# Transposing six of eight output blocks on VectorE and by transfers in SBUF, with the gate row in float32r and the norm's constant on GpSimd, in a fused linear-attention block

## The chip, the cores and the metric

One Trainium2 chip, one of its cores. The metric is the time of one execution on the device in microseconds (us), lower is better; a figure of a kernel is the median of its runs. The engines are TensorE (PE, with its weight loads shown apart as PEld), VectorE (DVE), ScalarE (ACT), GpSimd (POOL) and SyncE (SP), which issues nearly all transfers (DMAs).

## The reference

Sequence length, model width and number of rows are 1024 each, all data is float32, and there is one layer: a gated linear attention with a modulated RMS norm ahead of it.

```
c_act = silu(c)
shift, scale, gate = split(c_act @ ada_w + ada_b, 3)
h = rmsnorm(x, norm_g) * (1 + scale) + shift
q, k, v, g_lr, r = split(h @ w_in)            # 512, 512, 1024, 16, 1024 columns
log_a = log_sigmoid(g_lr @ w_alpha + b_alpha) / 16
o = chunked gated linear attention of q, k, v, log_a   # 4 heads of 256 values
o = rmsnorm(o, norm_g of the head) * silu(r)
x = x + gate * (o @ w_out)
return rmsnorm(x, final_g)
```

## The kernel before

Matrix products of float32 data are made of three float32r products: each operand is split into a rounded high part and the rest (`hi = Copy(x)` on ACT, `lo = x - hi` on DVE or POOL), and hi\*hi, hi\*lo and lo\*hi are accumulated (`PAIRS`, line 424). Most of the kernel's small engine work is such splitting.

The program has three stages. First the modulation, the transposed and split h (`hh0` to `hh7`, `hl0` to `hl7`, one pair for each 128 columns of h), and the projection to q and k. Then 32 steps, s = 0 to 31 (line 958): each is one tile of 128 rows times a quarter of the columns of v and r, 24 main matmuls of 512 columns (272 and 256 for s under 8, where the decay's columns ride along). Step s also carries, by `hooks` (line 881), pieces of the attention of earlier steps: chunk n = s - 4 of 128 rows of one head goes through `gla_at`, `gla_kv`, `gla_o` and `gla_og`; the exponentials of two chunks go through `e_head` to `e_kt`. Then 16 steps, s = 32 to 47, make the output: step 32 + t multiplies row tile t of o by the first half of w_out's columns, step 40 + t by the second, 24 main matmuls of 512 columns each (the last step in two halves), followed by the residual sum and the final norm.

o is collected in eight output blocks `OG[b]` of 128 x 4 x 256: block b holds four row tiles of one head, so head b // 2, rows 512 (b % 2) on. `gla_o` (line 797) sums a chunk's squares on ACT into `oss`, DVE multiplies by 1/256 and adds epsilon, POOL raises to the power -1/2 into `ors`, and `gla_og` (line 810) multiplies the chunk by that and by silu(r), which lies in the block already.

`o_tr(t)` (line 858) makes the transposed and split tile t for the output: eight 128x128 transposes on PE into two banks of PSUM, two copies of 512 columns on ACT (`hh`), two subtractions on DVE (`hl`). It overwrites `hh`t and `hl`t of the projection, which step 31 reads last, so it starts in step 31 at the earliest, and step 32 + t waits for it. Ahead of those steps w_out's pieces are loaded into `raw`, `wa` and `qk` slots, scaled on DVE by the head's norm weights and the gate row (`scale_piece`, line 616) and split (`conv_piece`).

The gate row `GB` (tile `wg`) is summed over eight pieces in 128 partitions by DVE; `gate_bc` (line 850) then sums over the partitions and spreads the row, with one full float32 matmul against a matrix of ones for each half, in steps 5 and 7, and a copy back on DVE.

The order of the instructions isn't that of the code: class `Program` collects them, gives each a latest start by estimated costs, and issues a list-scheduled order on each engine (`schedule`, line 129). Each engine then runs its list in that order. Almost every instruction is therefore recorded at line 217, and the rows are told apart by their tiles.

Of the kernel before, what the change touches and what calls it, by code (L numbers as in the profile page):

```python
# [8 lines left out]
F32R = mybir.dt.float32r  # L9
U8 = mybir.dt.uint8  # L10
AF = mybir.ActivationFunctionType
ALU = mybir.AluOpType
# [4 lines left out]
EPS = 1e-6  # L17
# [8 lines left out]
class Program:  # L26
# [37 lines left out]
    def cost(self, e, m, out, ins, kw):  # L64
        n = 1
        for d in out.shape[1:]:
            n *= d
        psum = any(a.space == bass.MemoryType.PSUM for a in ins + [out])
        if m == "dma_start":
            return n * out.shape[0] * 4 / 360e3  # L70
        if e == "pe":
            if m == "transpose":
                return 0.11
            k = 1 if ins[0].dtype == F32R else 4
            return 0.0135 + n * k / 2400 if n > 1 else 0.22
        if e == "act":
            return (0.05 if psum else 0.09) + n / 1200 + (0.2 if "accum_out" in kw else 0) + \
                (0.095 * sum(hasattr(kw.get(a, 0), "tensor") for a in ("scale", "bias")))
        if e == "dve":
            fast = m in ("tensor_copy", "tensor_scalar", "memset") and not psum  # L80
            return (0.13 if "scalar" in m else 0.068) + n * (0.52 if fast else 1.042) / 1000
        if m != "tensor_tensor":
            return 0.08 + n * 0.8 / 1000
        return 0.46 if kw.get("op") == ALU.pow else 0.11 + n * 2.1 / 1000
# [144 lines left out]
def gla_block(ctx, tc, x, c, ada_w, ada_b, norm_g, w_in, w_alpha, b_alpha, gn_g, w_out, final_g, out):  # L229
    nc = tc.nc  # L230
    prog = Program(nc)
# [220 lines left out]
    def gate_w_load():  # L452
# [5 lines left out]
        for q0 in (0, 32, 96):  # L458
            sync.dma_start(war[q0:q0 + 16, :], w_alpha[0])

    def gate_w_conv():
        war = W["a"]
        act.activation(WA, war, AF.Copy)
        dve.tensor_tensor(WA[32:64, :], war[32:64, :], f(WA[32:64, :]), op=ALU.subtract)
# [217 lines left out]
    oss = T("oss", [128, 32])  # L682
    ors = T("ors", [128, 32])

    OG, X, SHL, KD = {}, {}, {}, {}

    def c4(ap):
        return ap.rearrange("p (c i) -> p c i", i=64)
# [108 lines left out]
    def gla_o(n):  # L797
        u, s = n // 2, n % 2
        p = P(("m4", "m5")[n % 2 if n > 2 else 0])
        PO[n] = p  # L800
        inter = n % 8 != 0
        if inter:
            mm3(p[:, :256], [X[u][i][:, 640 + 128 * s:768 + 128 * s] for i in range(2)],
                [SHL[n][:, i, :] for i in range(2)], last=False)
        mm3(p[:, :256], ATH[n], vt(n), first=not inter)
        act.activation(p[:, 256:512], p[:, :256], AF.Square, accum_out=oss[:, n:n + 1])
        dve.tensor_scalar(oss[:, n:n + 1], oss[:, n:n + 1], 1.0 / 256, EPS, op0=ALU.mult, op1=ALU.add)
        pool.tensor_tensor(ors[:, n:n + 1], oss[:, n:n + 1], mh[:, 0:1], op=ALU.pow)

    def gla_og(n):  # L810
        og = OG[n // 4][:, n % 4, :]
        dve.scalar_tensor_tensor(og, PO[n][:, :256], ors[:, n:n + 1], og, op0=ALU.mult, op1=ALU.mult)

    def og_tag(b):
        return f"wa{12 + b}" if b < 2 else f"qk{b // 2 - 1}{1 - b % 2}"
# [29 lines left out]
    def gate_acc(i):  # L845
        kk, j = i // 2, i % 2
        g = GB[:, 512 * j:512 * j + 512]
        dve.scalar_tensor_tensor(g, GA[i], cact[:, kk:kk + 1], g, op0=ALU.mult, op1=ALU.add)

    def gate_bc(i):  # L850
        p = P("tr")
        pe.matmul(p, ones, GB[:, 512 * i:512 * i + 512], start=True, stop=True)
        dve.tensor_copy(GB[:, 512 * i:512 * i + 512], p)


    OT = {}

    def o_tr(t):
        oh = T(f"hh{t}", [128, 8, 128], F32R)
        ol = T(f"hl{t}", [128, 8, 128], F32R)  # L860
        OT[t] = (oh, ol)
        for g in range(2):
            p = P(("tr", "md")[g])
            for i in range(4):
                e = 4 * g + i
                src = OG[(e // 2) * 2 + t // 4][:, t % 4, 128 * (e % 2):128 * (e % 2) + 128]
                pe.transpose(p[:, 128 * i:128 * i + 128], src, ident)
            hi = oh[:, 4 * g:4 * g + 4, :].rearrange("p a b -> p (a b)")
            lo = ol[:, 4 * g:4 * g + 4, :].rearrange("p a b -> p (a b)")
            act.activation(hi, p, AF.Copy)  # L870
            dve.tensor_tensor(lo, p, f(hi), op=ALU.subtract)

    XRT = ["qk31", "G", "qk30", "wa7", "wa4", "wa5", "wa14", "wa8"]
    XR, FS = {}, {}
# [6 lines left out]
    def hooks(s):  # L881
        H = {}

        def at(k, fn, *a):
            H.setdefault(k, []).append((fn, a))
# [50 lines left out]
        if s < 5:  # L936
            for i in range(4):
                if s > 0:
                    at(i, gate_acc, 4 * (s - 1) + i)
                if s < 4:  # L940
                    at(4, gate_load, 4 * s + i)
            if s == 0:
                at(0, gate_init)
        if s == 5:
            at(0, gate_bc, 0)
        if s == 7:
            at(0, gate_bc, 1)
        if s >= 31 and s < 39:
            at(4 if s == 31 else 1, o_tr, s - 31)
        if s >= 32 and s < 40:  # L950
# [101 lines left out]
```

## Time and profile before

| | us |
|---|---|
| median of 3 runs (lowest to highest) | 454.27 (453.81 to 457.32) |
| the profiled execution, its own time | 455.46 |
| its span in the profile | 453.7 |

The span runs from the program's first recorded instruction to its last; 1.8 us lie outside it. The profile's page gives busy time by engine, the chain of work that ended last, and groups of instructions with their count, busy time and mean duration in ns. Views of the trace give the same for any stretch. A busy engine isn't the bound for that alone: what counts is what waits for what. Ends of matmuls are modelled, so the distance from one start to the next is the better measure of a matmul.

### The profile page before, as it was taken

The page shows a single profiled execution, that of the slowest core. Times are in us where ns is not written, and L with a number is a line of the kernel's source. Part 1 is how long each engine was busy: PE and PEld are TensorE (multiplying, and loading weights), DVE is VectorE, ACT ScalarE, POOL GpSimd, SP SyncE. Part 2 cuts the span into 40 slices and gives each one's busy share as a digit, 9 for nine tenths or more (in the row PEclk, how much of TensorE's full clock was granted, in tenths as well). Part 3 has the DMA queues.
Part 4 walks back from the last instruction along what each step waited for, and adds up shares of the span by engine and source line. Part 5 has one row for each costly group of instructions (what it writes and reads, how often), then busy time and mean ns, then how long its engine had stood idle before and what let it go on. Part 6 is the DMA issues. An engine that isn't in the chain of part 4 may idle for free.

```text
span 453.7 us, 6865 instructions
## 1 busy us (share of the span) xinstructions
PE 440.6 (97%) x2426; PEld 377.8 (83%) x2426; DVE 313.4 (69%) x704; ACT 245.9 (54%) x564; POOL 127.8 (28%) x147
## 2 busy tenths in 40 slices
PE   8799999999999999999999999999999999999994
PEld 8687778888999998888888888878888888888883
DVE  2698856165216889987797877998789976464433
ACT  4675869110136667658668486685859641351111
POOL 3100201020002326442373524726256420040001
PEclk9999999999999999999999999999999999999998
DMA  8999752068200103100140001300014525002222
GB/s 270 351 310 305 249 119 60 25 189 266 56 1 0 48 12 93 38 0 12 36 117 24 0 12 36 117 24 1 1 47 147 190 95 172 1 1 92 92 94 92
DMA packets 40063, 43.09 MB, mean 95 GB/s; under 512 B 3847, under 2 KB 32685, under 8 KB 40030
## 3 DMA queue, kind: packets, MB, share of 16 engines
q1 hardware_dynamic: 39982, 42.65, 29.9%
q8 instruction: 19, 0.31, 0.3%
q14 instruction: 14, 0.11, 0.1%
q10 hardware_dynamic: 48, 0.01, 0.0%
HBM read 38.46 MB, written 4.19 MB: 94 GB/s over the span
## 4 chain that ended last, share of the span: by engine, by line
PE 73%; DVE 13%; DMA 6%; ACT 3%; issue 3%; SPq 1%; POOL 0%; POOLq 0%; DVEq 0%; ACTq 0%
PE pm L217 65%; DVE wa L217 7%; PE pmd L217 5%; DMA qk<-in_ada_w 4%; PE ptr L217 3%; DVE Sf L217 2%; DMA raw<-in_gla_w_in 1%; SPq L217 1%; ACT wa L217 1%; DVE x L217 1%; DVE v L217 1%; DVE raw L217 1%; DVE ATf L217 1%; ACT hl L217 0%; DVE rs L217 0%
## 5 line engine op out<-in xcount | busy, mean ns | idle before, releaser
L217 PE MATMUL pm<-x,hh 128*128 128x512 f32 (+2 forms) x424 | 121.9, 370 | 0.0
L217 PE MATMUL pm<-wa,hh 128*128 128x512 f32 (+2 forms) x424 | 120.6, 368 | 0.0
L217 PEld LDWEIGHTS pm<-wa,hh 128*128 128x128 f32 x424 | 73.5, 188 | 10.5
L217 PEld LDWEIGHTS pm<-x,hh 128*128 128x128 f32 x424 | 71.8, 189 | 9.0 <-issue 1.0
L217 PE MATMUL pm<-wa,hl 128*128 128x512 f32 (+2 forms) x212 | 77.3, 365 | 0.0
L217 PE MATMUL pm<-x,hl 128*128 128x512 f32 (+2 forms) x212 | 77.1, 364 | 0.0
L217 ACT ACTIVATE wa<-wa 128x256 f32<-128x256 f32 (+4 forms) x126 | 59.7, 496 | 21.6 <-DVE wa L217 16.4
L217 PE MATMUL pm<-hh,wa 128*128 128x512 f32 (+1 forms) x236 | 62.1, 386 | 1.0 <-ACT hh L217 1.0
L217 PEld LDWEIGHTS pm<-hh,wa 128*128 128x128 f32 x236 | 41.7, 188 | 9.2 <-ACT hh L217 2.0
L217 POOL TENSOR_TENSOR wa<-wa,wa 128x896 fp32r<-128x896 f32 (+1 forms) x22 | 43.0, 1956 | 14.0 <-ACT wa L217 14.0
L217 PEld LDWEIGHTS pm<-wa,hl 128*128 128x128 f32 x212 | 39.8, 188 | 6.7
L217 PEld LDWEIGHTS pm<-x,hl 128*128 128x128 f32 x212 | 39.8, 188 | 6.3
L217 PE MATMUL pm<-wa,wa 128*128 128x256 f32 (+1 forms) x208 | 38.5, 281 | 0.1
L217 POOL TENSOR_TENSOR Shl<-Sf,Shl 128x256 fp32r<-128x256 f32 x28 | 23.0, 821 | 47.4 <-ACT Shl L217 47.4
L217 PEld LDWEIGHTS pm<-wa,wa 128*128 128x128 f32 x208 | 31.7, 189 | 4.6 <-DVE wa L217 1.1
L217 POOL TENSOR_TENSOR ors<-oss,mh 128x1 f32<-128x1 f32 x32 | 19.7, 615 | 52.0 <-DVE oss L217 52.0
L217 ACT ACTIVATE qk<-pm 128x256 f32<-128x256 f32 (+1 forms) x31 | 12.9, 424 | 39.3 <-PE pm L217 30.7
L217 PE MATMUL pm<-hl,wa 128*128 128x512 f32 (+1 forms) x118 | 32.9, 382 | 0.0
L217 DVE TENSOR_TENSOR wa<-pm,wa 128x256 fp32r<-128x256 f32 (+2 forms) x37 | 17.9, 483 | 17.7 <-PE pm L217 11.3
L217 DVE TENSOR_TENSOR wa<-wa 128x256 f32<-128x256 f32 (+1 forms) x48 | 24.1, 525 | 8.1 <-ACT wa L217 7.9
L217 POOL TENSOR_TENSOR D<-wa 128x256 f32<-128x256 f32 x16 | 11.7, 732 | 62.5 <-DVE wa L217 58.8
L217 ACT ACTIVATE pm<-wa 128x512 f32<-128x512 f32 (+1 forms) x11 | 6.2, 561 | 38.1 <-DVE wa L217 30.9
(175 smaller groups left out, 766.7 us busy)
## 6 DMA issues: line engine op xcount, KB each, us to landing
qk<-in_ada_w SPq DMA_DIRECT2D x32, 256.0 KB, 5.8
raw<-in_gla_w_in SPq DMA_DIRECT2D x48, 128.0 KB, 2.2
raw<-in_ada_w SPq DMA_DIRECT2D x16, 256.0 KB, 3.4
raw<-in_gla_w_in SPq DMA_DIRECT2D x8, 384.0 KB, 5.7
qk<-in_x SPq DMA_DIRECT2D x6, 512.0 KB, 5.2
wa<-in_x SPq DMA_DIRECT2D x5, 512.0 KB, 4.1
x<-in_x SPq DMA_DIRECT2D x4, 512.0 KB, 3.4
raw<-in_gla_w_out SPq DMA_DIRECT2D x8, 256.0 KB, 3.7
```

The lines of the kernel that those rows point to most:

```text
L217: getattr(self.eng[o["e"]], o["m"])(*o["call"][0], **o["call"][1])
```

## The change

Blocks 0 to 5 are transposed without PE. When a block's last chunk is done (`prog.hold` on `OGD`), DVE transposes its four tiles of 128x256 in blocks of 32x32 into a staging tile `oy`, of which there is one, and SP issues 16 transfers inside SBUF that put the 32x32 blocks where the whole transpose has them, into `O2[b]`, which takes the place of `OG[b]`. `o_tr` then reads three of four parts from `O2` and only the last head's (blocks 6 and 7) from two PE transposes; it copies and subtracts in four parts of 256 columns rather than two of 512. The gate row is split into hi and lo (`gate_split`: ACT and POOL), and each half is summed with two float32r matmuls against a float32r matrix of ones; both halves are now done in step 5. The norm's multiply and add moves from DVE to POOL. The planner is told that a transfer inside SBUF costs 0.6.

```diff
         if m == "dma_start":
-            return n * out.shape[0] * 4 / 360e3
+            return 0.6 if ins[0].tensor.name in self.acc else n * out.shape[0] * 4 / 360e3
...
+    onesr = T("onesr", [128, 128], F32R)
     def gate_w_conv():
+        dve.tensor_copy(onesr, ones)
...
-        dve.tensor_scalar(oss[:, n:n + 1], oss[:, n:n + 1], 1.0 / 256, EPS, op0=ALU.mult, op1=ALU.add)
+        pool.tensor_scalar(oss[:, n:n + 1], oss[:, n:n + 1], 1.0 / 256, EPS, op0=ALU.mult, op1=ALU.add)
...
+    def gate_split(i):
+        if i == 0:
+            GS[0] = T("wa6", [128, 2, 512], F32R)
+        g = GB[:, 512 * i:512 * i + 512]
+        act.activation(GS[0][:, 0, :], g, AF.Copy)
+        pool.tensor_tensor(GS[0][:, 1, :], g, f(GS[0][:, 0, :]), op=ALU.subtract)
+
     def gate_bc(i):
         p = P("tr")
-        pe.matmul(p, ones, GB[:, 512 * i:512 * i + 512], start=True, stop=True)
+        for j in range(2):
+            pe.matmul(p, onesr, GS[0][:, j, :], start=j == 0, stop=j == 1)
         dve.tensor_copy(GB[:, 512 * i:512 * i + 512], p)
...
+    def o_blocks(b, i):
+        if i == 0:
+            OY[b] = T("oy", [128, 4, 8, 32])
+        y = OY[b]
+        prog.hold(dve.transpose(y[:, i].rearrange("p e i -> p (e i)"), OG[b][:, i, :]), OGD[4 * b + 3])
+        if i < 3:
+            return
+        O2[b] = T(og_tag(b), [128, 4, 2, 128])
+        yv = y.rearrange("p t (g c) i -> p t g c i", c=4)
+        for c in range(4):
+            for r in range(4):
+                sync.dma_start(O2[b][32 * c:32 * c + 32, :, :, 32 * r:32 * r + 32],
+                               yv[32 * r:32 * r + 32, :, :, c, :])
...
     def o_tr(t):
...
-        for g in range(2):
-            p = P(("tr", "md")[g])
-            for i in range(4):
-                e = 4 * g + i
-                src = OG[(e // 2) * 2 + t // 4][:, t % 4, 128 * (e % 2):128 * (e % 2) + 128]
-                pe.transpose(p[:, 128 * i:128 * i + 128], src, ident)
-            hi = oh[:, 4 * g:4 * g + 4, :].rearrange("p a b -> p (a b)")
-            lo = ol[:, 4 * g:4 * g + 4, :].rearrange("p a b -> p (a b)")
-            act.activation(hi, p, AF.Copy)
-            dve.tensor_tensor(lo, p, f(hi), op=ALU.subtract)
+        p = P(("tr", "md")[t % 2])
+        for i in range(2):
+            pe.transpose(p[:, 128 * i:128 * i + 128], OG[6 + t // 4][:, t % 4, 128 * i:128 * i + 128], ident)
+        for g in range(4):
+            hi = oh[:, 2 * g:2 * g + 2, :].rearrange("p a b -> p (a b)")
+            lo = ol[:, 2 * g:2 * g + 2, :].rearrange("p a b -> p (a b)")
+            src = O2[2 * g + t // 4][:, t % 4].rearrange("p a b -> p (a b)") if g < 3 else p[:, 0:256]
+            act.activation(hi, src, AF.Copy)
+            dve.tensor_tensor(lo, src, f(hi), op=ALU.subtract)
...
+        if s == 4:
+            at(4, gate_split, 0)
         if s == 5:
             at(0, gate_bc, 0)
-        if s == 7:
-            at(0, gate_bc, 1)
+            at(0, gate_split, 1)
+            at(4, gate_bc, 1)
+        if s % 4 in (1, 2) and 8 <= s <= 30:
+            for i in range(2):
+                at((2, 6)[i], o_blocks, s // 4 - 2, 2 * (s % 4 - 1) + i)
```

The planner's list moves with it. DVE in step 31, before: `x` and `wa` are w_out's pieces being split and parts of the attention, `hl` the output tile's low part.

```order
L217 TENSOR_TENSOR x_489_552<-raw_455_518,x_489_552 128x512
L217 TENSOR_SCALAR oss_284<-oss_284 128x1
L217 COPY_PREDICATED ATf_207_270<-mask_267,pm_488_551 64x128
L217 COPY_PREDICATED ATf_207_270<-mask_267,pm_488_551 64x64
L217 SCALAR_TENSOR_TENSOR qk_441_504<-pm_487_550,ors_285,qk_441_504 128x256
L217 CAST wa_212_275<-ATf_207_270 128x128
L217 TENSOR_TENSOR wa_209_272<-pmd_553,wa_209_272 128x256
L217 TENSOR_TENSOR x_491_554<-raw_456_519,x_491_554 128x512
L217 TENSOR_TENSOR hl_494_557<-ptr_558,hh_493_556 128x512
L217 TENSOR_TENSOR wa_214_277<-ATf_207_270,wa_212_275 128x128
L217 TENSOR_TENSOR hl_494_557<-pmd_559,hh_493_556 128x512
```

The same place after it, where `wa_326`, `qk_396` and `qk_471` are the transposed blocks 0, 2 and 4:

```order
L217 TENSOR_TENSOR hl_508_571<-wa_326_389,hh_507_570 128x256
L217 TENSOR_TENSOR hl_508_571<-qk_396_459,hh_507_570 128x256
L217 COPY_PREDICATED ATf_208_271<-mask_268,pm_502_565 64x128
L217 COPY_PREDICATED ATf_208_271<-mask_268,pm_502_565 64x64
L217 TENSOR_TENSOR x_505_568<-raw_467_530,x_505_568 128x512
L217 CAST wa_213_276<-ATf_208_271 128x128
L217 TENSOR_TENSOR hl_508_571<-ptr_572,hh_507_570 128x256
L217 TENSOR_TENSOR wa_215_278<-ATf_208_271,wa_213_276 128x128
L217 TENSOR_TENSOR wa_210_273<-pmd_567,wa_210_273 128x256
L217 TENSOR_TENSOR x_512_575<-raw_469_532,x_512_575 128x512
L217 TENSOR_TENSOR hl_508_571<-qk_471_534,hh_507_570 128x256
```

Two subtractions from PSUM became four, three of which read SBUF alone, and the multiply and add on `oss` is gone. The four scalings of w_out's second half, which stood between the subtractions of the third and fourth output tiles, now stand behind those of the fifth.

DVE in step 25, where w_out's first half is scaled (`raw`, `wa` with `wg`), before:

```order
L217 TENSOR_TENSOR wa_213_276<-ATf_206_269,wa_211_274 128x128
L217 SCALAR_TENSOR_TENSOR qk_375_438<-pm_435_498,ors_285,qk_375_438 128x256
L217 SCALAR_TENSOR_TENSOR raw_455_518<-raw_455_518,cols_20_83,wg_286 128x512
L217 SCALAR_TENSOR_TENSOR raw_456_519<-raw_456_519,cols_20_83,wg_286 128x512
L217 SCALAR_TENSOR_TENSOR raw_457_520<-raw_457_520,cols_20_83,wg_286 128x512
L217 SCALAR_TENSOR_TENSOR raw_458_521<-raw_458_521,cols_20_83,wg_286 128x512
L217 COPY_PREDICATED ATf_207_270<-mask_267,pm_444_507 64x128
```

And after, with block 4's transposes (`oy`):

```order
L217 SCALAR_TENSOR_TENSOR qk_381_444<-pm_445_508,ors_286,qk_381_444 128x256
L217 TENSOR_TENSOR wa_214_277<-ATf_207_270,wa_212_275 128x128
L217 STREAM_TRANSPOSE oy_518<-qk_381_444 128x256 x4
L217 SCALAR_TENSOR_TENSOR raw_466_529<-raw_466_529,cols_20_83,wg_287 128x512
L217 SCALAR_TENSOR_TENSOR raw_467_530<-raw_467_530,cols_20_83,wg_287 128x512
L217 SCALAR_TENSOR_TENSOR raw_468_531<-raw_468_531,cols_20_83,wg_287 128x512
L217 TENSOR_TENSOR v_218_281<-pm_442_505,v_218_281 128x256
```

The four transposes came in ahead of the scalings, and the fourth scaling moved to the next step.

SP's list from the third quarter of w_in's columns to w_out's first loads, before:

```order
L217 DMA qk_349_412<-in_gla_w_in 128x256 x4
L217 DMA raw_407_470<-in_gla_w_in 128x256 x2
L217 DMA raw_408_471<-in_gla_w_in 128x256 x2
L217 DMA raw_409_472<-in_gla_w_in 128x256 x2
L217 DMA raw_410_473<-in_gla_w_in 128x256 x2
L217 DMA wa_411_474<-in_gla_w_in 128x256 x4
L217 DMA qk_415_478<-in_gla_w_in 128x256 x4
L217 DMA raw_455_518<-in_gla_w_out 128x512
```

And after, where the groups of 16 are the transfers inside SBUF:

```order
L217 DMA qk_354_417<-in_gla_w_in 128x256 x4
L217 DMA wa_359_422<-oy_405 32x8x32 x16
L217 DMA raw_416_479<-in_gla_w_in 128x256 x2
L217 DMA raw_417_480<-in_gla_w_in 128x256 x2
L217 DMA raw_418_481<-in_gla_w_in 128x256 x2
L217 DMA raw_419_482<-in_gla_w_in 128x256 x2
L217 DMA wa_420_483<-in_gla_w_in 128x256 x4
L217 DMA qk_396_459<-oy_448 32x8x32 x16
L217 DMA qk_424_487<-in_gla_w_in 128x256 x4
L217 DMA qk_429_492<-oy_475 32x8x32 x16
L217 DMA raw_466_529<-in_gla_w_out 128x512
```

The weight loads keep their order, and three groups of 16 stand between them; the last of these groups is now ahead of w_out's first load.

## Rows read from the trace of the kernel before

**Rows 1.** The page: span, and busy time of each engine.

```profile
span 453.7 us, 6865 instructions
PE 440.6 (97%) x2426; PEld 377.8 (83%) x2426; DVE 313.4 (69%) x704; ACT 245.9 (54%) x564; POOL 127.8 (28%) x147
```

**Rows 2.** Chain that ended last, 372 to 395 us: start us, us, what.

```profile
380.22 5.52 PE pm L217 x24
385.74 0.44 PE ptr L217 x4
386.18 0.44 PE pmd L217 x4
...
```

**Rows 3.** Timeline of PE in steps 5 and 7: start us, us, instruction, count.

```profile
150.44 1.02 PE L217 MATMUL ptr<-wg,ones 128*128 128x512 f32 x2
...
151.54 0.29 PE L217 MATMUL pm<-x,hl 128*128 128x272 f32 x1
...
168.47 0.41 PE L217 MATMUL pm<-x,hh 128*128 128x272 f32 x2
168.72 0.29 PE L217 MATMUL pm<-x,hl 128*128 128x272 f32 x1
```

**Rows 4.** Windows, steps 9, 25, 31-34, 37: length; busy PE, PEld, DVE, ACT, POOL; clock.

```profile
181.60:188.80 7.20, 7.20 (x40) 6.13 (x39) 6.82 (x19) 5.80 (x16) 2.68 (x4) 1.00 0.19 57
...
294.80:301.80 7.00, 7.00 (x37) 5.91 (x36) 6.92 (x16) 5.44 (x12) 1.28 (x3) 1.00 0.13 47
...
337.70:345.70 8.00, 8.00 (x47) 6.87 (x46) 7.47 (x17) 7.60 (x19) 6.09 (x5) 1.00 0.12 38
345.70:353.70 8.00, 8.00 (x47) 6.83 (x46) 7.83 (x19) 6.97 (x16) 3.07 (x4) 1.00 0.68 226
353.70:361.80 8.10, 8.10 (x48) 6.95 (x47) 8.05 (x17) 5.99 (x15) 3.62 (x3) 1.00 0.56 197
361.80:369.60 7.80, 7.80 (x46) 6.70 (x44) 7.44 (x20) 2.63 (x8) 2.31 (x3) 1.00 0.23 67
...
384.20:390.60 6.40, 6.40 (x34) 5.35 (x33) 3.84 (x7) 1.70 (x4) 0.00 (x0) 1.00 0.11 45
```

**Rows 5.** Groups by line and form: count, busy us, mean ns, idle before.

```profile
L217 ACT ACTIVATE hh<-ptr 128x512 fp32r<-128x512 f32 x8 | 4.7, 591 | 1.6 <-PE ptr L217 1.6
L217 ACT ACTIVATE wa<-raw 128x256 fp32r<-128x256 f32 x8 | 3.2, 415 | 3.4 <-DMA raw<-in_gla_w_in 3.3
L217 DVE TENSOR_TENSOR hl<-ptr,hh 128x512 fp32r<-128x512 f32 x8 | 5.5, 686 | 1.2 <-ACT hh L217 1.1
L217 DVE TENSOR_TENSOR wa<-raw,wa 128x256 fp32r<-128x256 f32 x8 | 3.3, 420 | 2.9 <-ACT wa L217 2.9
L217 DVE TENSOR_TENSOR_SCAN wa<-rs,wa 128x256 f32<-128x256 f32 x16 | 12.9, 806 | 0.3
L217 DVE TENSOR_SCALAR oss<-oss 128x1 f32<-128x1 f32 x32 | 4.7, 148 | 3.3 <-ACT pm L217 2.8
L217 DVE SCALAR_TENSOR_TENSOR raw<-raw,cols,wg 128x512 f32<-128x512 f32 x8 | 7.5, 970 | 0.0
L217 POOL TENSOR_SCALAR ss<-ss 128x1 f32<-128x1 f32 x4 | 1.1, 282 | 11.7 <-ACT hl L217 11.7
```

**Rows 6.** Timeline of DVE in steps 31 and 32: start us, us, instruction.

```profile
341.95 1.33 DVE L217 CAST wa<-ATf 128x128 fp32r<-128x128 f32 x1
...
351.30 0.22 DVE L217 CAST wa<-ATf 128x128 fp32r<-128x128 f32 x1
```

**Rows 7.** Timeline of PE in step 26: the idle time before, and what ended it.

```profile
303.31 0.44 PE L217 MATMUL pmd<-ident,D 128*128 128x128 f32 x2 [0.41 <-DVE D L217]
```

**Rows 8.** Timeline of SP, and the page's DMA issues (KB, us to landing).

```profile
213.84 2.97 SPq L217 DMA_DIRECT2D qk<-in_gla_w_in  x4
...
292.99 0.80 SPq L217 DMA_DIRECT2D wa<-in_gla_w_out  x2
...
qk<-in_gla_w_in SPq DMA_DIRECT2D x12, 128.0 KB, 2.3
```

More of the change, by code (lines that the diff above doesn't have):

```diff
@@ L683, in gla_block @@
     ors = T("ors", [128, 32])
-    OG, X, SHL, KD = {}, {}, {}, {}
+    OG, X, SHL, KD, OGD = {}, {}, {}, {}, {}
     def c4(ap):
@@ L811, in gla_og @@
         og = OG[n // 4][:, n % 4, :]
-        dve.scalar_tensor_tensor(og, PO[n][:, :256], ors[:, n:n + 1], og, op0=ALU.mult, op1=ALU.mult)
+        OGD[n] = dve.scalar_tensor_tensor(og, PO[n][:, :256], ors[:, n:n + 1], og, op0=ALU.mult, op1=ALU.mult)
     def og_tag(b):
@@ L848, in gate_acc @@
         dve.scalar_tensor_tensor(g, GA[i], cact[:, kk:kk + 1], g, op0=ALU.mult, op1=ALU.add)
+    GS = {}
+    def gate_split(i):
[4 more added lines that the diff above has]
+        pool.tensor_tensor(GS[0][:, 1, :], g, f(GS[0][:, 0, :]), op=ALU.subtract)
     def gate_bc(i):
         p = P("tr")
-        pe.matmul(p, ones, GB[:, 512 * i:512 * i + 512], start=True, stop=True)
+        for j in range(2):
+            pe.matmul(p, onesr, GS[0][:, j, :], start=j == 0, stop=j == 1)
         dve.tensor_copy(GB[:, 512 * i:512 * i + 512], p)
     OT = {}
+    def o_blocks(b, i):
[11 more added lines that the diff above has]
+                               yv[32 * r:32 * r + 32, :, :, c, :])
+    OY = {}
+    O2 = {}
     def o_tr(t):
```

## The prediction

> **What bounds the kernel now.** I read the head of the page first: TensorE (PE) is busy for 440.6 of 453.7 us, VectorE (DVE) for 313.4, ScalarE (ACT) for 245.9 [rows 1]. A busy PE need not be a bound PE, so I then read the chain of waits late in the program. It lists nothing but PE: 24 matmuls in 5.52 us, four transposes in 0.44, and four more in 0.44 [rows 2]. There PE goes from one instruction to the next without waiting, so what is taken from its list shortens the end by its own length, as long as the engines that feed it keep up. Whether they do I read from the windows, cut at the first matmul of each step of 24 main matmuls. In the four steps from 337.7 to 369.6 us PE is busy all the time, but DVE is close behind: 7.47 of 8.0 us, 7.83 of 8.0, 8.05 of 8.1, 7.44 of 7.8. ACT has 7.60 and 6.97 in the first two [rows 4]. So PE sets the end by a narrow margin: DVE and ACT are the ones to watch.
>
> **The change, part by part.**
>
> 1. The transposes leave PE. Of 64 transposes (8 in each of steps 31 to 38) 48 go. Four take 0.44 us [rows 2], one 0.11, so 48 x 0.11 = 5.28 us. They stand between main matmuls on an engine that doesn't wait, so I count them in full, 0.66 per step.
>
> 2. The gate row. Before, from the start of one gate matmul (150.44) to the third main matmul behind it (151.54) it is 1.10 us; two such main matmuls take 0.25 (168.47 to 168.72), which leaves 0.85 for the gate matmul in full float32 [rows 3]. Now it is two float32r matmuls of the same 512 columns, each at 5.52 / 24 = 0.23 [rows 2]: 0.46. Two gate halves: 2 x 0.39 = 0.78 us less. The new splits (two copies on ACT, two subtractions on POOL) and the cast of the ones are charged nothing: they are issued a step ahead of the matmul, at a place where, as the windows of the neighbouring steps go, ACT and POOL have idle time. If that cover fails, a late split holds PE for about one POOL subtraction.
>
> 3. ACT's evacuations. A step had two copies of 512 columns at 0.591; it has four of 256, from SBUF for three of them, at 0.415 (a copy of that size from SBUF): 4 x 0.415 - 2 x 0.591 = +0.48 us [rows 5]. In steps 31 and 32 ACT then has 7.60 + 6.97 + 0.96 = 15.5 us of work [rows 4], and the two steps without their transposes last 16.0 - 1.3 = 14.7. The 0.8 us too many is my charge for this place. Below it could be nothing, because copies for later steps can be put off; in the order they are put ahead instead. From step 33 on ACT has room.
>
> 4. DVE's subtractions. A step had two of 512 columns from PSUM at 0.686; it has four of 256 at 0.42 (two operands in SBUF): +0.31 a step [rows 5]. The norm's constant goes to POOL, 0.148 less for each chunk. The order also moves four scalings of the second half of w_out (0.97 each, 3.9 in all) from steps 33 and 34 to behind the fifth output block's subtractions. For steps 31 to 34: 30.8 + 1.2 - 0.6 - 3.9 = 27.5 us of DVE work, in 31.9 - 2.6 = 29.3 us. That fits, so I charge nothing; rival A says what happens when it doesn't.
>
> A row that bears on this: the same cast of 128x128 took 0.22 us at 351.30 and 1.33 at 341.95 [rows 6], the longer one where POOL is at its busiest (6.09 of 8.0 [rows 4]). [...]
>
> 5. The DVE transposes, 24 of 128x256. The trace has none. The nearest rows are a subtraction of the same size at 0.42 and, dearer, a scan of that size at 0.806; the cheap end is DVE's smallest row, 0.148 [rows 5]. I take 0.42, the row of the same size. Four make 1.7 us per block. Blocks 1, 2, 3 and 5 fall on steps where DVE has idle time. Block 0 falls near step 9, where DVE has 6.82 of 7.2 us, block 4 on step 25 with 6.92 of 7.0 [rows 4]; there one scaling is moved out in exchange (0.97). Too much work: 6.82 + 1.68 - 0.15 - 7.2 = 1.15 and 6.92 + 1.68 - 0.97 - 0.15 - 7.0 = 0.5, together 1.6. DVE works somewhat ahead of PE and the next steps have room, so I charge a third, 0.5. By the dear end (0.806) it is 2.7 + 2.0 = 4.7, by the cheap end 0.
>
> 6. The norm's constant on POOL: the nearest row is 0.282 (a tensor_scalar of 128x1 on POOL), then the power as before. Nobody near waits for it: the scaled output has more than a step until its transpose. DVE no longer stands behind ACT's square. No charge; a gain of DVE's few waits is in rival C.
>
> 7. The 96 transfers on SP. In the order each group of 16 stands between weight loads. A transfer costs SP 0.40 (two in 0.80) to 0.74 us (four in 2.97), and loads of this size land in 2.3 [rows 8]. A block is then 16 x 0.40 + 2.3 = 8.7 us, at the dear end 14.1. The loads queued behind were issued tens of us before they are used, and the last block's outputs are read in step 35. I charge nothing.
>
> **The sum.** -5.28 - 0.78 + 0.8 + 0.5 = -4.76 us. The profiled execution took 455.46 us, 1.8 more than its span; the sum gives 450.7 for one like it. The median of the runs is 454.27, 1.2 below the profiled one, and against it the sum gives 449.5.
>
> **The rivals.**
>
> A. DVE becomes the bound in steps 31 to 35. For it: the windows (94% in the sum of part 4), and the stretched cast. If each of the 12 new SBUF subtractions of those steps meets POOL at work (POOL is busy for 15.1 of 31.9 us there, 47% [rows 4]) and then loses 1.1 us (1.33 - 0.22), DVE has 12 x 0.47 x 1.1 = 6.2 us more: 33.7 in 29.3, 4.4 too late, 453.9. With half of it, 31 - 29.3 = 1.3 too late, 450.8. Against: the subtractions of later blocks can run ahead, and PE reads the pieces in the order in which they come. I take 452.5, nearer to the worst than to the half.
>
> B. Slower: one staging buffer and an engine that issues in order. The first transpose of a block waits on DVE until all 16 transfers of the block before have landed, and everything behind it on DVE, then PE, waits too. The tightest place is from block 3's last transpose (step 22) to block 4's first (step 25): 3 steps of about 7 us, 21 us. It decides from (21 - 2.3) / 16 = 1.2 us per transfer, 1.6 times the dear end of [rows 8]. At 1.6 us a block takes 27.9: DVE is held for 7 us there and for some less at the other blocks, whose scalings and weight loads stand behind it too. About +10 on the forecast: 460. Against: SP's rows. Pieces of 128 bytes, 4096 per block, are in no row.
>
> [...]
>
> C. More than the sum: nothing is lost at the hand-overs, and PE also sheds waits such as the 0.41 us for DVE at 303.31 [rows 7]. -6.06 - 0.41 gives 447.8.
>
> D. It doesn't do what it says: the transposes only filled time in which PE would have waited, as DVE's load suggests. Then the gate's 0.78 is left, 453.5. Against: step 37 lasts 6.40 with DVE at 3.84 [rows 4], and is longer than 5.52 by just its transposes [rows 2].
>
> **How the numbers follow.** Forecast 0.53 (own range 447.9 to 451.5), A 0.27, B 0.08, C 0.10, D 0.02. One per cent, about what a measurement of this kernel can tell from no change, is 4.5 us, so faster by over 1% means below 449.7. The forecast lies next to that line: 0.32 of its 0.53 fall below, with C that makes 0.42. The rest of it (0.21), A and D stay within 1%: 0.50. B is the slower side: 0.08. The range takes in C's side down to 447.4 and A with its worst price and a little more, up to 454.4; B is left out.
>
> **What would show it.** Right: steps 37 and 38 at 5.74 us (6.40 - 0.66), all eight steps from 31 on shorter by about 0.66 except 31 and 32; a gate matmul pair in 0.46; no wait of PE over 0.5 us behind step 8; DVE transposes near 0.42. Wrong by A: steps 32 to 35 at 7.8 us or more with DVE at the step's length, subtractions of 128x256 over 0.6 on average. Wrong by B: DVE idle ahead of a transpose with a transfer as the releaser, SP over 1 us per transfer. If transposes on DVE take 0.8, the loss sits at steps 9 to 11 and 25 to 27 as waits of PE for DVE.

## The result and the profile after

The changed kernel takes 448.60 us (median of 4 runs, 447.56 to 449.24) against 454.04 before (median of 4): ratio 0.9869, 95% interval 0.9846 to 0.9892, so 1.3% faster, and by more than 1% over the whole interval. The forecast was 449.5, range 447.4 to 454.4. The profiled execution took 449.24 us, 6.2 less than the one of before; the medians differ by 5.4.

The head of the page after, against [rows 1]:

```profile
span 447.5 us, 6956 instructions
PE 436.2 (97%) x2378; PEld 375.6 (84%) x2378; DVE 321.8 (72%) x713; ACT 247.1 (55%) x582; POOL 142.5 (32%) x181
```

PE has 48 instructions fewer (2426 to 2378): the 48 transposes. The gate's matmuls make four records in both traces, since one in full float32 is recorded as two ([rows 3], x2). DVE and POOL do more, by 8.4 and 14.7 us.

Where the time went is read by steps. Each is measured from its first main matmul to that of the next, in both profiled executions:

| steps | before, us | after, us | difference |
|---|---|---|---|
| up to step 1 | 124.24 | 123.92 | -0.32 |
| 1 to 4 | 25.12 | 25.12 | 0 |
| 5 to 7 (gate row) | 24.39 | 23.67 | -0.72 |
| 8 | 7.83 | 7.38 | -0.45 |
| 9, 10 (block 0 on DVE) | 14.28 | 15.52 | +1.24 |
| 11 to 25 | 105.96 | 105.84 | -0.12 |
| 26 | 8.09 | 7.28 | -0.81 |
| 27 to 30 | 27.77 | 27.83 | +0.06 |
| 31 to 38 (transposes) | 59.31 | 54.48 | -4.83 |
| 39 to the end | 56.76 | 56.48 | -0.28 |

The sum is -6.2 us, as the spans have it. Most of it is where the forecast had it, and two places are not in the forecast's sum: steps 8 and 26 shed waits (-1.26), and steps 9 and 10 lost 1.24.

The windows after, of steps 9, 10, 26, 31 to 34 and 37 (length; then busy time of PE, PEld, DVE, ACT, POOL; clock, DMA share, GB/s), against [rows 4]:

```profile
180.10:187.60 7.50, 7.36 (x39) 6.07 (x38) 6.93 (x20) 5.33 (x17) 2.88 (x5) 1.00 0.32 65
187.60:195.60 8.00, 7.37 (x38) 6.10 (x37) 6.13 (x14) 3.47 (x12) 4.27 (x5) 1.00 0.22 35
301.50:308.70 7.20, 7.20 (x40) 6.21 (x39) 7.12 (x17) 4.10 (x13) 4.07 (x4) 1.00 0.28 45
336.60:344.00 7.40, 7.40 (x42) 6.26 (x41) 6.96 (x15) 7.40 (x21) 4.86 (x5) 1.00 0.31 87
344.00:351.30 7.30, 7.30 (x41) 6.23 (x40) 7.30 (x12) 7.28 (x24) 5.39 (x6) 1.00 0.60 203
351.30:358.60 7.30, 7.30 (x40) 6.10 (x39) 7.18 (x22) 7.19 (x16) 2.37 (x4) 1.00 0.26 85
358.60:366.20 7.60, 7.60 (x41) 6.17 (x40) 7.49 (x21) 4.96 (x17) 3.82 (x4) 1.00 0.60 202
379.50:385.30 5.80, 5.80 (x28) 4.69 (x27) 3.21 (x7) 1.00 (x3) 0.00 (x0) 1.00 0.21 80
```

In step 10 PE is idle for 0.63 of 8.0 us, and there DVE isn't short of time: it is busy for 6.13. In steps 31 to 34 PE never stops, but DVE is busy for 28.9 of 29.6 us and ACT for 21.9 of the first 22.0.

The groups that answer to [rows 5] (count, busy us, mean ns, idle before):

```profile
L217 DVE STREAM_TRANSPOSE oy<-qk 128x256 f32<-128x256 f32 x16 | 6.0, 416 | 0.0
L217 DVE TENSOR_TENSOR hl<-qk,hh 128x256 fp32r<-128x256 f32 x16 | 7.7, 503 | 0.1
L217 DVE TENSOR_TENSOR hl<-wa,hh 128x256 fp32r<-128x256 f32 x8 | 5.1, 638 | 0.0
L217 DVE TENSOR_TENSOR hl<-ptr,hh 128x256 fp32r<-128x256 f32 x4 | 1.7, 422 | 0.2
L217 ACT ACTIVATE hh<-qk 128x256 fp32r<-128x256 f32 x16 | 6.2, 412 | 0.0
L217 POOL TENSOR_SCALAR oss<-oss 128x1 f32<-128x1 f32 x32 | 9.7, 302 | 35.9 <-ACT pm L217 34.8
```

A block transpose on DVE takes 0.416 us, ACT's copy 0.412, POOL's multiply and add 0.302, all within 0.02 of what was taken for them. The subtractions tell more: with an operand in PSUM 0.422, with both in SBUF 0.503 and 0.638.

Step 10 shows why. DVE around the wait (start us, us, instruction), then POOL, then PE:

```profile
187.56 2.20 DVE L217 TENSOR_TENSOR wa<-ATf,wa 128x128 fp32r<-128x128 f32 x1
```

```profile
187.50 2.10 POOL L217 TENSOR_TENSOR wa<-wa,wa 128x896 fp32r<-128x896 f32 x1 [2.75 <-ACT wa L217]
```

```profile
189.81 0.39 PE L217 MATMUL pm<-wa,wa 128*128 128x256 f32 x1 [0.63 <-DVE wa L217]
```

DVE's subtraction of 128x128, 0.28 us elsewhere, began 0.06 us behind a long POOL subtraction, ended 0.15 us after it, and PE waited for its result. The busy share counts all 2.20 us as busy, 1.92 more than this work takes elsewhere. In the kernel before the same two instructions met in the same step, and PE did not wait. DVE, then PE, in step 10 of that kernel:

```profile
189.19 1.98 DVE L217 TENSOR_TENSOR wa<-ATf,wa 128x128 fp32r<-128x128 f32 x1
```

```profile
189.94 0.40 PE L217 MATMUL pm<-wa,wa 128*128 128x256 f32 x2
190.18 0.62 PE L217 MATMUL pm<-x,hh 128*128 128x512 f32 x2
190.64 0.40 PE L217 MATMUL pm<-x,hl 128*128 128x512 f32 x1
190.88 0.63 PE L217 MATMUL pm<-x,hh 128*128 128x512 f32 x2
191.34 0.28 PE L217 MATMUL pm<-wa,wa 128*128 128x256 f32 x1
```

DVE was not earlier there: its subtraction ended 2.39 us behind the first matmul of the step (188.78), in the changed kernel 2.14 us behind it (187.62). PE's list differs. The last of the three matmuls `pm<-wa,wa` needs the result; before, five main matmuls stand ahead of it, and in the changed kernel it follows the other two at once. So the wait takes two things, the hold, which both kernels have, and the place of that matmul in PE's list. Whether block 0's transposes have a part in it, the experiments tell.

### The profile page after: what moved, and what is told of

Read it like the earlier page. It is cut to its first block, busy times and chain, and to the rows that moved or that the text cites. A ratio compares the mean times of both kernels' runs of the same rounds, so it can differ in the third digit from the quotient of the medians.

```text
span 447.5 us, 6956 instructions
## 1 busy us (share of the span) xinstructions
PE 436.2 (97%) x2378; PEld 375.6 (84%) x2378; DVE 321.8 (72%) x713; ACT 247.1 (55%) x582; POOL 142.5 (32%) x181
## 4 chain that ended last, share of the span: by engine, by line
PE 80%; DVE 8%; ACT 5%; issue 2%; POOL 2%; DMA 1%; SPq 1%; POOLq 0%; DVEq 0%; ACTq 0%
PE pm L217 71%; PE pmd L217 6%; DVE wa L217 5%; PE ptr L217 4%; ACT wa L217 2%; DMA qk<-in_ada_w 1%; ACT L216 1%; ACT qk L217 1%; DVE Sf L217 1%; POOL ors L217 1%; SPq L217 1%; DVE ATf L217 1%; DVE oy L217 1%; POOL D L217 1%; ACT pm L217 0%
## 5 line engine op out<-in xcount | busy, mean ns | idle before, releaser
L217 PE MATMUL pm<-hh,wa 128*128 128x512 f32 (+1 forms) x236 | 64.3, 399 | 0.0
L217 PEld LDWEIGHTS pm<-hh,wa 128*128 128x128 f32 x236 | 44.2, 203 | 7.3
L217 DVE TENSOR_TENSOR wa<-ATf,wa 128x128 fp32r<-128x128 f32 (+1 forms) x36 | 25.3, 703 | 1.0 <-ACT wa L217 0.7
L217 PEld LDWEIGHTS pm<-hl,wa 128*128 128x128 f32 x118 | 22.4, 197 | 4.2
```

Source lines behind the costliest of these rows:

```text
L217: getattr(self.eng[o["e"]], o["m"])(*o["call"][0], **o["call"][1])
```

## The experiments

The kernel before ran beside each of them, at 453.92 to 454.20 us. Steps are counted by their first matmuls.

### The three parts, each alone

The gate row alone (x_gate), on the kernel before:

```diff
+        act.activation(GS[0][:, 0, :], g, AF.Copy)
+        pool.tensor_tensor(GS[0][:, 1, :], g, f(GS[0][:, 0, :]), op=ALU.subtract)
...
-        pe.matmul(p, ones, GB[:, 512 * i:512 * i + 512], start=True, stop=True)
+        for j in range(2):
+            pe.matmul(p, onesr, GS[0][:, j, :], start=j == 0, stop=j == 1)
```

> The kernel before with the gate row's float32r sums alone. By the term of the prediction (two gate halves, 0.39 us each) steps 5 to 7 together last 23.6 to 23.8 us against 24.4, and nothing else moves: the total is 0.6 to 0.8 us below before. Rival: the new splits on ACT and POOL come late or stretch DVE, PE waits for them, and steps 5 to 7 last 24.2 us or more: total within 0.2 us of before.

Measured: 454.10 us, ratio 0.9996 (0.9986 to 1.0006). Steps 5 to 7 last 23.85 us, 0.55 less than before; step 8 gives 0.13 back. The rest is below what these runs can tell. So the term is real but 0.55, not 0.78. The price of a pair is not what is missing. PE of x_gate at its second pair:

```profile
155.93 0.63 PE L217 MATMUL ptr<-wa,onesr 128*128 128x512 f32 x2
156.39 0.28 PE L217 MATMUL pmd<-wa,hl 128*128 128x256 f32 x1
```

From 155.93 to 156.39 the pair takes 0.46 us, as was forecast, and the first pair takes 0.47. Step 7, which has no gate matmul any more, loses its 0.85. The rest is lost in step 5: it lasts 8.27 us, and 7.95 before, less 0.85 and plus two pairs, makes 8.03. In this step PE transposes D, the decayed k, and DVE makes D behind two subtractions. DVE before, then DVE, POOL and PE in x_gate:

```profile
152.45 0.76 DVE L217 TENSOR_TENSOR wa<-wa 128x256 f32<-128x256 f32 x2
```

```profile
152.07 1.87 DVE L217 TENSOR_TENSOR wa<-wa 128x256 f32<-128x256 f32 x2
```

```profile
152.31 1.48 POOL L217 TENSOR_TENSOR wa<-wg,wa 128x512 fp32r<-128x512 f32 x1
```

```profile
154.01 0.29 PE L217 MATMUL pm<-wa,hl 128*128 128x272 f32 x1
154.34 0.44 PE L217 MATMUL ptr<-ident,D 128*128 128x128 f32 x2
```

The new split on POOL (`wg`) held up the second of the two, 1.1 us, and the transposes of D start 0.32 us behind the matmul ahead of them, where 0.12 is usual. That is the rival's "stretch DVE", at a smaller price than it named. In the changed kernel the first pair takes 0.47 us and the second 0.57, because its second matmul comes 0.1 us late.

The norm's constant alone (x_norm), on the kernel before:

```diff
-        dve.tensor_scalar(oss[:, n:n + 1], oss[:, n:n + 1], 1.0 / 256, EPS, op0=ALU.mult, op1=ALU.add)
+        pool.tensor_scalar(oss[:, n:n + 1], oss[:, n:n + 1], 1.0 / 256, EPS, op0=ALU.mult, op1=ALU.add)
```

> The kernel before with the norm's constant on POOL alone. By the prediction's charge (nothing) the total moves by less than 0.4 us and the wait of PE in step 26 (step of 8.09 us) stays. Rival: this edit is what shed PE's waits in the changed kernel, so step 26 falls from 8.1 to about 7.3 us and step 8 from 7.8 to 7.4: total 0.8 to 1.3 us less.

Measured: 454.99 us, ratio 1.0019 (1.0005 to 1.0034), a little slower. Both expectations were wrong in the total, and the rival was right about its two places: step 8 falls from 7.83 to 7.28 us, step 26 from 8.09 to 7.36. But step 31 rises from 8.06 to 9.63. DVE and POOL in that step of x_norm:

```profile
343.58 1.64 DVE L217 TENSOR_TENSOR x<-raw,x 128x512 fp32r<-128x512 f32 x1
345.25 0.42 DVE L217 TENSOR_TENSOR wa<-pmd,wa 128x256 fp32r<-128x256 f32 x1
345.59 0.68 DVE L217 TENSOR_TENSOR hl<-ptr,hh 128x512 fp32r<-128x512 f32 x1
```

```profile
342.55 2.12 POOL L217 TENSOR_TENSOR wa<-wa,wa 128x896 fp32r<-128x896 f32 x1
344.63 1.73 POOL L217 TENSOR_TENSOR x<-raw,x 128x512 fp32r<-128x512 f32 x1
```

A subtraction of 128x512 with both operands in SBUF (0.68 us elsewhere) ended 0.55 us behind POOL's long one, and the subtraction behind it, which frees the PSUM bank that PE wants, came late: PE waited 1.3 us for it.

The blocks alone (x_blocks): the changed kernel with both other parts undone.

```diff
-        pool.tensor_scalar(oss[:, n:n + 1], oss[:, n:n + 1], 1.0 / 256, EPS, op0=ALU.mult, op1=ALU.add)
+        dve.tensor_scalar(oss[:, n:n + 1], oss[:, n:n + 1], 1.0 / 256, EPS, op0=ALU.mult, op1=ALU.add)
...
-            pe.matmul(p, onesr, GS[0][:, j, :], start=j == 0, stop=j == 1)
+        pe.matmul(p, ones, GB[:, 512 * i:512 * i + 512], start=True, stop=True)
```

> The kernel before with the six blocks transposed by DVE and transfers alone (gate row and norm's constant as before). Steps 31 to 38 last 54.3 to 54.8 us against 59.3, that is 4.5 to 5.0 less, if the gain there is the transposes'. If the waits of PE in steps 9 and 10 of the changed kernel come from block 0's transposes on DVE, they are here too, 0.8 to 1.5 us; if they come from the work on POOL that the norm's constant brought, they are gone. Total 3.2 to 4.2 us below before in the first case, 4.5 to 5.0 in the second.

Measured: 451.62 us, ratio 0.9934 (0.9908 to 0.9961). Steps 31 to 38 last 55.80 us, 3.5 less than before and 1.3 more than in the changed kernel, nearly all of it in step 32 (8.41 against 7.29): there a cast of 128x128 was held for 2.15 us beside POOL's long subtraction. Step 26 keeps its 8.09. Steps 9 and 10 lose only 0.24. So block 0's transposes alone do not make the wait in step 10: the subtraction there is held (2.00 us), but PE's list has its five main matmuls in between, as before. With the gate row alone or the norm's constant alone two stand in between, and step 10 lasts 7.18 and 7.23 us (7.08 before). The parts don't add: alone they give -0.1, +0.8 and -2.6 us, -1.8 in all, and together -5.4 (before in these runs 454.17). Each part shifts the lists a little, and with it which DVE instruction stands beside a long POOL instruction.

### The wait in steps 9 and 10

Block 0 later (x_late):

```diff
-OGD[4 * b + 3])
+OGD[4 * b + (3 if b else 6)])
...
+                if s > 11:
                     at((2, 6)[i], o_blocks, s // 4 - 2, 2 * (s % 4 - 1) + i)
+        if s == 12:
+            for i in range(4):
+                at(i, o_blocks, 0, i)
```

> The changed kernel with block 0's four DVE transposes moved from step 8 to behind chunk 6's output (step 11 to 12). If the 0.8 and 0.3 us that PE waits in steps 9 and 10 come from DVE being 1.4 us later by these transposes, steps 9 and 10 last 14.2 to 14.6 us against 15.5, the waits there are under 0.2, and the total is 0.8 to 1.3 us less than the changed kernel's. Rival: the wait comes from the POOL instruction that holds up a DVE subtraction for 2.2 us in step 10, whatever stood before it: the wait stays at 0.5 us or more, and the total is within 0.4 us of the changed kernel's.

Measured: 452.11 us, ratio 0.9953 (0.9936 to 0.9970), slower than the changed kernel by 3.5. Step 9 lasts 7.17 us (7.52 in the changed kernel): its part of the loss goes with the transposes. Step 10 lasts 7.88, as good as unchanged (8.00): the rival holds there, with a hold of 2.18 us and the three matmuls in a row. And step 32 now takes 9.5 us, after a scaling that was held in step 31:

```profile
342.47 2.31 DVE L217 SCALAR_TENSOR_TENSOR qk<-qk,cols,wg 128x512 f32<-128x512 f32 x1
```

```profile
342.10 2.13 POOL L217 TENSOR_TENSOR wa<-wa,wa 128x896 fp32r<-128x896 f32 x1 [0.43 <-ACT wa L217]
```

POOL's long subtractions in four pieces (x_split):

```diff
-        pool.tensor_tensor(xl, XF[:, 0:896], f(xh), op=ALU.subtract)
+        for a in range(0, 896, 224):
+            pool.tensor_tensor(xl[:, a:a + 224], XF[:, a:a + 224], f(xh[:, a:a + 224]), op=ALU.subtract)
```

> The changed kernel with POOL's 16 subtractions of 128x896 (2.1 us each) cut into four of 224 columns. If a DVE instruction with its inputs in SBUF waits for the POOL instruction that is under way to end (in the changed kernel a subtraction of 128x128 is held for 2.2 us in step 10), no DVE instruction of that size takes over 0.9 us beside these pieces, the wait of PE in step 10 (0.8 us) is gone, and the total is 0.5 to 1.5 us less than the changed kernel's. Rival: DVE only shares a path with POOL and loses as much to four short instructions as to one long: DVE's busy time (321.8 us) and PE's wait in step 10 stay, total within 0.4 us, or more by POOL's added time.

Measured: 450.81 us, ratio 0.9920 (0.9897 to 0.9943). What the theory, that DVE waits for the whole POOL instruction, says of DVE holds: steps 9 and 10 fall from 15.5 to 14.34 us, with no wait left there, and DVE's busy time falls though it has the same 713 instructions, while POOL's rises. The page of x_split:

```profile
PE 437.2 (98%) x2378; PEld 375.0 (84%) x2378; DVE 308.0 (69%) x713; ACT 249.1 (56%) x582; POOL 155.4 (35%) x229
```

308.0 against 321.8 us. What it says of the total fails: 2.2 us slower than the changed kernel. In the new order PE waits elsewhere: 1.0 us in two pieces for D in steps 17 and 34, and 0.8 for a split in steps 18 and 26. Steps 17, 26 and 34 last 7.84, 8.39 and 8.41 us (6.95, 7.28 and 7.63 in the changed kernel).

The same subtractions on DVE (x_subdve):

```diff
-        pool.tensor_tensor(xl, XF[:, 0:896], f(xh), op=ALU.subtract)
+        dve.tensor_tensor(xl, XF[:, 0:896], f(xh), op=ALU.subtract)
```

> The changed kernel with these 16 subtractions of 128x896 on DVE instead of POOL. DVE gets 16 x 1.1 = 18 us of work (128x768 takes 0.95). If each of them on POOL holds up DVE by some 1.9 us, DVE's busy time falls or stays (321.8 us + 18 - up to 30), PE's waits behind step 8 are under 0.5 us together, and the total is 0.5 to 1.5 us less than the changed kernel's. Rival: what counts is the work on DVE: its busy time rises by 15 us or more, steps 31 to 34 become longer than 7.3 to 7.6 us, and the total is 2 to 6 us more.

Measured: 449.44 us, ratio 0.9902 (0.9880 to 0.9923). With 16 more instructions of 1.19 us (19.0 in all) DVE is busy for 316.4 us, 5 less than in the changed kernel; steps 9 and 10 last 14.25. The rival (work on DVE counts) falls. The total is 1 us more than the changed kernel's, not less: step 26 takes 8.71 us and step 34 8.13, with PE waiting for D (1.1 us in three pieces behind step 8).

Both together (x_late_sub): block 0 late and the subtractions on DVE.

> The run with block 0 moved late, and POOL's subtractions of 128x896 on DVE as well. With block 0 late, step 31 took 9.5 us against 7.4 in the changed kernel, while a scaling on DVE took 2.3 us next to such a subtraction on POOL. If it was held by it, step 31 is at 7.4 to 7.7 us here and steps 9 and 10 at 14.2 together, so that the total is 447 to 449 us. Rival: the block moved late leaves DVE with more to do in step 31 than fits, whatever POOL does: step 31 stays at 9 us or more, and the total at 450.5 or more.

Measured: 449.91 us, ratio 0.9903 (0.9884 to 0.9923). What the expectation calls step 31 of the run with block 0 late is, counted by matmuls, step 32; here both last 7.40 and 7.29 us, and steps 9 and 10 14.25. So both waits go with POOL's long subtraction. The total missed again: steps 26 and 34 take 8.69 and 8.16, and PE waits for D for 1.2 us in three pieces.

### The transfers

Twice as many, half as large (x_dma32). The planner was told half the price of each, so that the lists stayed in place:

```diff
-                sync.dma_start(O2[b][32 * c:32 * c + 32, :, :, 32 * r:32 * r + 32],
-                               yv[32 * r:32 * r + 32, :, :, c, :])
+                for h in (slice(0, 2), slice(2, 4)):
+                    sync.dma_start(O2[b][32 * c:32 * c + 32, h, :, 32 * r:32 * r + 32],
+                                   yv[32 * r:32 * r + 32, h, :, c, :])
```

> The changed kernel with each of the 96 transfers cut in two of half the size, in the same place and order on every engine. A transfer takes SP 0.65 us now, a block 16 x 0.65 + 1.9 = 12.3 us, and the tightest place, block 1's last transpose to block 2's first, is 19.9 us. If SP's time is per transfer, a block takes 32 x 0.65 + 1.9 = 22.7 us, DVE is held for about 3 us ahead of blocks 2 and 4, and the total is 2 to 6 us more than the changed kernel's: rival B's mechanism, with its point of decision at 1.1 us per transfer. If SP's time goes by the pieces moved (4096 per block in both), a half takes about 0.33 us and nothing changes: within 0.4 us.

Measured: 461.75 us (457.35 to 463.25), ratio 1.0148 (1.0095 to 1.0201): 13 us more than the changed kernel where 2 to 6 were expected, and slower than before. SP of the changed kernel (block 0), then of x_dma32 (block 1): start, us, count:

```profile
181.40 11.40 SPq L217 DMA_DIRECT2D wa<-oy  x16
```

```profile
216.76 21.37 SPq L217 DMA_DIRECT2D wa<-oy  x32
```

A transfer costs SP 0.65 to 0.71 us whether it has 32 KB or 16. The waits of DVE in x_dma32 between 236 and 310 us (total, times, longest) show what follows:

```profile
DVE oy L217 <- DMA qk<-oy: 6.2, 2, 3.9
DVE oy L217 <- DMA wa<-oy: 3.2, 1, 3.2
```

The first transpose of a block waits for the staging tile, and DVE, ACT and PE wait behind it: steps 18, 21, 25, 26 and 34 last 0.8, 2.2, 3.0, 2.1 and 1.8 us longer than in the changed kernel, 9.9 in all. That is rival B, made true. The profiled execution is the fastest of the four (457.35); what the other three lose beyond it, some 4 us, isn't settled. The planner's new line for such transfers plays no part in this case: without it every engine's list is the same.

### ACT in steps 31 to 34

Eight more copies (x_actpad):

```diff
             act.activation(hi, src, AF.Copy)
+            if t < 4 and g < 2:
+                act.activation(hi, src, AF.Copy)
```

> The changed kernel with 8 more copies of 128x256 on ACT (two parts of each of the first four output tiles are copied twice), 3.3 us in steps 31 to 34. In steps 31 to 33 ACT has 21.9 of 22.0 us of work now. If that work is due there, as the prediction's charge of 0.8 us for these steps has it, steps 31 to 34 get longer by 2 to 3 us. If much of it is done ahead of need, PE waits for less than 0.8 us in all and the total is within 0.8 us of the changed kernel's.

Measured: 448.08 us (2 runs), ratio 0.9872 (0.9848 to 0.9896). Steps 31 to 34 last 29.78 us against 29.66. The windows of these steps in x_actpad (columns as above):

```profile
335.30:342.70 7.40, 7.40 (x42) 6.26 (x41) 6.74 (x15) 7.40 (x22) 4.83 (x5) 1.00 0.32 89
342.70:350.00 7.30, 7.30 (x40) 6.19 (x39) 7.27 (x13) 7.28 (x25) 4.92 (x6) 1.00 0.57 189
350.00:357.20 7.20, 7.20 (x39) 6.10 (x39) 7.02 (x21) 7.13 (x15) 2.07 (x4) 1.00 0.29 101
357.20:365.10 7.90, 7.84 (x42) 6.17 (x41) 7.82 (x21) 7.52 (x25) 4.37 (x5) 1.00 0.54 179
```

In the first three ACT is as full as before, and the added work has pushed other work into step 34 (7.52 us, from 4.96). PE hardly notices: much of what ACT does in these steps is ahead of need.

### A version that beats both?

All split subtractions on DVE (x_subdve2): x_subdve, and for the weight pieces

```diff
-        eng = pool if kt in (2, 4, 6) else dve
-        eng.tensor_tensor(w[:, 1, :], r, f(w[:, 0, :]), op=ALU.subtract)
+        dve.tensor_tensor(w[:, 1, :], r, f(w[:, 0, :]), op=ALU.subtract)
```

> As the run before it, and the subtractions of 128x512 of every weight piece on DVE as well (14 or so, 0.68 us on DVE against 1.3 to 1.7 on POOL). By the theory that POOL's instructions hold up DVE: step 31 to 34 keep 7.3 us or less and the total is 0.5 to 2 us less than the changed kernel's. Rival (work on DVE counts): steps 31, 32 and the last of each column quarter get longer by 2 us each, total 4 to 10 us more.

Measured: 449.06 us, ratio 0.9884 (0.9863 to 0.9904). DVE is busy for 313.6 us with 34 instructions more than in the changed kernel. The rival falls, but the gain isn't there either: in steps 17, 25 and 33 (8.13, 8.11 and 8.26 us) PE waits for D, 2.1 us in all.

The changed kernel again (x_again), and beside it D's subtraction on DVE too (x_sub3):

```diff
-        pool.tensor_tensor(kd.rearrange("p (s i) -> p s i", s=2),
+        dve.tensor_tensor(kd.rearrange("p (s i) -> p s i", s=2),
```

> The changed kernel once more, beside the next one, for a comparison on one chip: 447.5 to 449.5 us.

> The changed kernel with the split subtractions of 128x896 and of 128x512 on DVE, as in the run before last but one, and also the subtraction of 128x256 that makes D (0.72 us on POOL, 0.42 on DVE, 16 of them). In that earlier run PE waited three times 0.8 to 0.9 us for D, in steps 17, 25 and 33, where D's subtraction stood on POOL behind the norm's constant and a power that took 1.4 us. If POOL's queue and the lock are what is late there, these three waits are under 0.3 us each and the total is 446 to 447.5 us, 1 to 2.5 less than the changed kernel's. Rival: with all this work DVE itself is the bound (some 320 us busy); the waits stay or move to other steps, total 448.5 us or more.

Measured: 448.34 us for x_again, ratio 0.9875 (0.9859 to 0.9892), every step from 1 on within 0.05 us of the first profile of the changed kernel; 448.33 for x_sub3, ratio 0.9872 (0.9854 to 0.9891). Steps 17 and 25 fall to 7.47 and 7.35 us, as the theory says (its lock is POOL's hold on DVE, as in the 2.20 us of step 10 above); step 33 stays at 8.45, with a wait of 0.8 us for D, which stands behind output-tile work on ACT and DVE. POOL is down to this in x_sub3:

```profile
PE 433.4 (97%) x2378; PEld 372.9 (84%) x2378; DVE 312.7 (70%) x763; ACT 249.6 (56%) x582; POOL 75.1 (17%) x131
```

It equals the changed kernel; no run beat it. DVE has 50 instructions more and 9 us less busy time, so the held-up time can be had back, but in these orders a wait for D took it. A hand-set place for D's chain in steps 25 and 33 wasn't tried.

## Why the prediction was right

**What bounds the kernel.** PE from end to end: right, and with little to spare. The sign "no wait over 0.5 us behind step 8" failed at one place, the 0.63 us in step 10.

**Part 1, the transposes** (-5.28): steps 31 to 38 are 4.83 shorter. Steps 37 and 38 last 5.77 and 5.75 against the 5.74 that were named, 0.63 less instead of 0.66. The rest is lost in steps 33 and 34 (-0.94 instead of -1.32), in gaps of 0.1 us or less between short and long matmuls; two transposes of D moved from step 33 to 34, which changes nothing in the two together.

**Part 2, the gate row** (-0.78): 0.55 by x_gate, and steps 5 to 7 of the changed kernel are 0.72 shorter. The price of the pair was right (0.46 and 0.47 in x_gate for 0.46). The step that failed is that the new splits were charged nothing. Their result was not late; POOL's subtraction held DVE for 1.1 us, and PE waited for D. The part looked for idle time on POOL and not at what DVE did beside it.

**Part 3, ACT** (+0.8 in steps 31 and 32): nothing. Both steps lost their full 0.66. The step that failed read a full window as a due one; x_actpad shows that 3.3 us more don't matter. "Below it could be nothing" was the right end.

**Part 4, DVE's subtractions** (nothing): right in time, but with a margin of 0.7 us (28.9 of 29.6) where 1.8 was worked out (27.5 of 29.3). The subtractions average (16 x 0.503 + 8 x 0.638) / 24 = 0.55 us, between the 0.42 taken and the 0.6 from which rival A was to be read.

**Part 5, the DVE transposes** (+0.5): the price was right (0.416 for 0.42), the place half right. Block 4 costs nothing; step 26 even gets shorter. At block 0 the loss is 1.24 us, near the 1.15 worked out there, but by luck, and not for its reason. The 0.92 in step 10 stays when the transposes leave (7.88 us in x_late) and goes when POOL's long subtraction leaves, with the transposes in place (7.06 in x_split, 7.07 in x_subdve). It is the hold and the new place of a matmul in PE's list. The 0.32 in step 9 goes either way (7.17 in x_late, 7.18 in x_subdve), so how much of it is too much work on DVE stays open.

**Part 6, the norm's constant** (no charge): this step failed in both directions. It costs POOL 0.30, as the row said, but it isn't neutral: it takes 1.28 us of waits out of steps 8 and 26, and alone it puts 1.57 into step 31. "Nobody near waits for it" looked at its own result; what it moves is the order of the lists.

**Part 7, the transfers** (no charge): right. 0.65 to 0.71 us each and 1.9 to land make 12.3 to 13.3 us per block, inside the 8.7 to 14.1.

**The sum** gave -4.76; the medians show -5.4 (x_again -5.6). The difference is part 3's 0.8, which wasn't there. That the other errors cancel is luck: parts 1 and 2 brought 0.5 less in the changed kernel, steps 9 and 10 cost 0.7 more than part 5's charge, and the waits shed in steps 8 and 26 gave 1.3.

**Rival A** did not decide the changed kernel, but the hold that it priced at 1.1 us is there. Half of its charge came: of the 12 new subtractions with both operands in SBUF, four were held in steps 31 to 34 (0.69 to 1.85 us instead of 0.42, 3.1 us more in all, against 6.2 for all that meet POOL). The two dearest:

```profile
346.30 1.51 DVE L217 TENSOR_TENSOR hl<-qk,hh 128x256 fp32r<-128x256 f32 x1
362.05 1.85 DVE L217 TENSOR_TENSOR hl<-wa,hh 128x256 fp32r<-128x256 f32 x1
```

A's reckoning lost 1.3 us to PE for that half; PE waited for none of it. The two rows from which the prediction took A's price (0.22 and 1.33 us) are of a cast, which has one operand, and it charged that price to subtractions with two; that these are held was not shown by its rows. Both kinds are held, up to 2.15 and 2.26 us, as the last section shows. In x_norm, x_blocks and x_late the hold took 1.6, 1.1 and 2.2 us in steps 31 and 32, the places that it named; that the changed kernel pays nothing there is the luck of its order (the cast held for 2.15 us in x_blocks is held as long here). That no PE wait remains in steps 31 to 34 could not have been read from the trace of before. **Rival B** was rightly kept small for its price (0.65 us against a point of decision at 1.2; by the trace after it is (19.9 - 1.9) / 16 = 1.1, from block 1's last transpose to block 2's first), and x_dma32, with two transfers of 0.65 in place of one, loses the 9.9 us, where 10 were worked out for 1.6. **Rival C** came half true, by shed waits. **D** is out: steps 31 to 38 shrank by the transposes.

## What to carry to other kernels

A full window is no due date: to learn whether an engine is late, look for who waits for it, or give it more work and see. When one engine holds up another, a change on either is worth what the new order of the lists makes of it: the same hold of 2 us cost nothing where PE asked for the result five matmuls later, and 0.9 us where it asked at once. So look at the list of the engine that waits as well as at that of the one that is late. Parts measured alone (-0.1, +0.8, -2.6) don't sum to the whole (-5.4), so a term of a few tenths in such a place needs a bound of a microsecond or two. Where a long instruction on one engine stalls short ones on another, moving it to the busier engine can lower that engine's load: 16 subtractions more on DVE made DVE less busy (x_subdve, 316.4 us for 321.8).

## What the runs showed of the hardware

In these traces DVE is held by POOL for as long as POOL's instruction lasts, and which DVE instructions are held differs by kind. In the changed kernel, subtractions of 128x128 with both operands in SBUF take 1.12 us on average when they start beside a POOL instruction (16 of them, up to 2.26) and 0.28 when not (16); casts of 128x128 from SBUF, with one operand, 1.06 (10, up to 2.15) and 0.22 (23). What holds them are POOL's wide subtractions (128x256 to 128x896): the 11 subtractions that took 0.70 us or more ended 0.14 to 0.15 us behind the one they had met, the 7 casts that took 0.35 or more 0.08 to 0.09 behind it. Beside POOL's instructions of 128x1 the subtractions took 0.28 to 0.29 us (4 of the 16) and the casts 0.23 (2 of the 10). Subtractions of 128x256 from PSUM take 0.416 in both cases (22 and 34), and block transposes, from SBUF with one operand, 0.428 (6, all beside subtractions of 128x256) and 0.414 (18). Four pieces of 224 columns in place of 896 (x_split) gave DVE 13.8 us back.

A transfer inside SBUF costs its issuer 0.65 to 0.71 us at 32 KB (10.39 to 11.41 us for the 16 of a block) and 0.67 at 16 KB (21.37 for 32, x_dma32), in pieces of 128 bytes: here the number of transfers sets the price, not their bytes or pieces.
